# Scan levels further apart in TensorE's order, value weights moved by 192 bytes, one pair of unread products taken out

## The chip, the core and the metric

The kernel runs on one core of a Trainium2 chip. The metric is the device time of one execution in microseconds (us). TensorE (PE) multiplies; VectorE (DVE), ScalarE (ACT) and GpSimd (POOL) do the rest; SyncE (SP) issues most of the DMAs.

## What is computed

One layer of an encoder on a sequence of 512 tokens with 1024 channels, all in float32:

```python
h = rms_norm(x, norm1_g)
u_pool, aq, ak, av, rq, rf, rb, ri, rg, gate_pre = split_cols(h @ w_in)
y_pool = pool_mixer(u_pool)                      # centred means over 2, 4, 8, 16 tokens
y_attn = diff_attention(aq, ak, av, lam)         # 4 heads
y_rec  = hgrn2_mixer(rq, rf, rb, ri, rg)         # two-way gated linear recurrence, 4 heads
x = x + (gates * (y @ w_up), summed over the three) @ w_out
h2 = rms_norm(x, norm2_g)
x = x + (silu(h2 @ w_gate) * (h2 @ w_up)) @ w_ffn_out
out = rms_norm(x, final_norm_g)
```

## The kernel before

**Products.** Every operand of a large product is split into a high and a low part of type float32r (`whi`, `wlo`, `hT_hi`, `hT_lo`), and a product is three terms. Two forms matter here. `cols_mm` holds weights still and streams 512 tokens of hT past them (512 columns in each matmul). `rows_mm` holds hT still and streams 256 columns of weights; it serves the *value* products, `ri` for the recurrence (tile v_rec) and `av` for the attention (va_hi, va_lo). The weights come by DMA into `raw`, are rounded by ACT into `whi` (L180) and subtracted by DVE into `wlo` (L181); both tiles come from the pool `wsp`, three buffers of 4096 bytes each. In the built program's layout the buffers of `wsp` and the tiles of hT begin at the same byte counted modulo 256, namely 32. In the feed-forward layer pads of 192 bytes ahead of the tiles put the streamed operand (the tiles of h2 and of its forms) at 224 and the weights at 32, so the two differ by 64 modulo 256.

**The scan.** `rec_scan(h)` computes one head of the recurrence as a pyramid of levels n = 1, 2, 4, ... 256. At each level PE makes four small float32 products (`rc<-kq,kc`, each two instructions in the trace), then two DVE multiplications (L755) change the queries of `kq` in place, POOL (L758; DVE at the level 128) changes its keys, ACT copies the keys (`kc`, L724), and DVE writes the level's products into the triangle `pt` under a mask (L770). A level's products need the multiplications of the level before.

**What sets the order.** PE's order is fixed when the program is written: `Pipe.run` lets generators yield, counts a nominal PE time for each matmul, and resumes a stream when its nominal time has come. A level of the scan yields ("w", 2.0) or ("w", 1.7): PE is to do that much other work (the projections in `jobs`) before the next level. The heads of the attention wait in the same way for the event AF (their queries and keys are there) and 3.5 more. The other engines' order is made by a scheduler from dependences and its own estimates; they run their queues in order.

**Unread products.** In the feed-forward layer each pair of column blocks j = 1 to 21 is seven products of half size with 256 columns in each matmul. After the first of them the pairs 4 and 12 issue two matmuls of 512 columns into a PSUM bank that nobody reads; the second streams the same weights from 64 bytes further on.

Of the kernel before, what the change touches and what calls it, by code (L numbers as in the profile page):

```python
# [11 lines left out]
F32 = mybir.dt.float32  # L12
# [6 lines left out]
P = 128  # L19
# [57 lines left out]
def encoder_kernel(ctx: ExitStack, tc: tile.TileContext, x, norm1_g, w_in, pool_w, pool_scale,  # L77
# [30 lines left out]
    const = ctx.enter_context(pool("const"))  # L108
    wraw = ctx.enter_context(pool("wraw", 2))
    wsp = ctx.enter_context(pool("wsp", 3))  # L110
    small = ctx.enter_context(pool("small", 6))
    psum = ctx.enter_context(pool("psum", 3, space=PSUM))

    def bank(name, shape=(P, 512)):
# [13 lines left out]
    mhalf = const.tile([P, 8], F32, name="mhalf")  # L128
    nc.vector.memset(mhalf, -0.5)
    masks = const.tile([P, len(LEVELS), P], U8, name="masks")  # L130
    vecs = const.tile([14, P], F32, name="vecs")
    vcol = const.tile([P, 14], F32, name="vcol")
    gain_a = const.tile([P, 1], F32, name="gain_a")
    lb = const.tile([P, 8], F32, name="lb")
# [28 lines left out]
    class Part:  # L163


        def __init__(self, chunk, view, a, b, wpool=None):
            self.chunk, self.view, self.a, self.b, self.wpool = chunk, view, a, b, wpool
            chunk.left += 1

        def ready(self):  # L170
            return True

        def split(self):
            self.hi, self.lo = split_w(self.view(self.chunk.raw), self.a, self.b, self.wpool)
            self.chunk.left -= 1

    def split_w(view, a, b, wpool=None):
        hi = (wpool or wsp).tile([P, a, b], F32R, name="whi")
        lo = (wpool or wsp).tile([P, a, b], F32R, name="wlo")
        nc.scalar.copy(out=hi, in_=view)  # L180
        nc.vector.tensor_tensor(out=lo, in0=view, in1=hi.bitcast(F32), op=ALU.subtract)  # L181
        return hi, lo
# [203 lines left out]
            for j in range(0, n, 2):  # L386
                yield Part(ch, lambda raw, j=j: raw[:, j:j + 2, :], 2, 512, wpool)

    def quarter_parts(w, c0, n, where=None):

        v = w.rearrange("(kt p) c -> p kt c", p=P)
        for c in range(0, n, 256):
            ch = Chunk(v[:, :, c0 + c:c0 + c + 256], KT, 256, where if c == 0 else None)
            yield slice(c, c + 256), [Part(ch, lambda raw, j=j: raw[:, j:j + 4, :], 4, 256) for j in (0, 4)]


    def cols_mm(ps, part, r, nk, sub=0, lo_col=0, n=512, r_lo_last=False):
# [68 lines left out]
    xg = st0.enter_context(pool("xg"))  # L466
    xraw = st0.enter_context(pool("xraw", 3))
    g_b = xg.tile([P, D], F32, name="g1b")
    with tc.issue_after(warmed):
        nc.scalar.dma_start(out=g_b, in_=norm1_g.broadcast_to([P, D]))  # L470
    xt, first_raw = [], []
# [237 lines left out]
    def rec_scan(h):  # L709
# [30 lines left out]
        while n < 256:  # L740
            nb2 = S // (2 * n)
            ps = bank("rc", (P, NB, P))
            for b in range(NB):
                if n <= 64:
                    ks = kc[:, b * P:(b + 1) * P]
                    qs = strided(kq, b * P, [[2 * n, P // (2 * n)], [S + n, 2], [1, n]])
                else:
                    ks = kq[:, 2 + b % 2, b * P:(b + 1) * P]
                    qs = kq[:, 1 - b % 2, (b ^ 1) * P:((b ^ 1) + 1) * P]
                mm(ps[:, b, :], ks, qs, True, True)  # L750

            for off, o in ((0, tstep + 1), (S + n, 0)):
                xv = strided(kq, off, [[2 * n, nb2], [1, n]])
                tv = strided(tot, toff + o, [[2, nb2], [0, n]])
                nc.vector.tensor_tensor(out=xv, in0=xv, in1=tv, op=ALU.mult)  # L755
            xv = strided(kq, 2 * S, [[2 * n, nb2], [S + n, 2], [1, n]])
            tv = strided(tot, toff + 1, [[2, nb2], [tstep - 1, 2], [0, n]])
            (nc.gpsimd if n < 128 else nc.vector).tensor_tensor(out=xv, in0=xv, in1=tv, op=ALU.mult)  # L758
            if n < 64:
                kc = key_copy(2 * n)  # L760
            if n < 128:
                pv = strided(pyr, poff, [[S, 2], [1, nb2]])
                a = strided(tot, toff, [[tstep, 2], [2, nb2]])
                c = strided(tot, toff + 1, [[tstep, 2], [2, nb2]])
                nc.vector.tensor_tensor(out=pv, in0=a, in1=c, op=ALU.mult)
                tot, toff, tstep = pyr, poff, S
                poff += nb2
            if n <= 64:
                m = masks[:, LEVELS.index(n), :].rearrange("p (o t) -> p o t", o=1).to_broadcast([P, NB, P])
                nc.vector.copy_predicated(out=diag, mask=m, data=ps)  # L770
            else:
                nc.scalar.copy(out=strided(pt, P, [[2 * S + 2 * P, 2], [S - P, 2], [1, P]]), in_=ps)
            n *= 2
            yield ("w", 2.0 if n <= 128 else 1.7)
        for d in range(2):
            ps = bank("rc", (P, 2, 256))
            ts = slice(256 * (1 - d), 256 * (1 - d) + 256)
# [17 lines left out]

    cols = {n: col_parts(w_in2, KT, OFF[n] + P, 512 - P, P) for n in ("rq", "rf", "rb")}
    cols["rg"] = col_parts(w_in2, KT, OFF["rg"], 512, P)
    vparts = list(quarter_parts(w_in2, OFF["ri"], 512))

    def add_front(h):  # L800
        for i, n in enumerate(("rq", "rf", "rb")):
# [56 lines left out]
    def att_head(h):  # L858
        if h:
            yield ("e", f"T{h - 1}", 0.0)  # L860
        yield ("e", f"AF{h}", 3.5)
        t = att.pop(h)
        at, (vh, vl), aT, y_attn = ATT["at"], ATT["v"], ATT["aT"], ATT["y"]
        strip = ATT["strip"].tile([P, 896], F32, name="strip")
        nc.sync.dma_start(out=strip, in_=c_dist[h])
        zz = at.tile([P, NB, 2], F32, name="zz")
        rr = at.tile([P, NB, 2], F32, name="rr")
        probs = {}

        def scores(i):  # L870
            bs = slice(i * P, (i + 1) * P)
            mx = small.tile([P, 2], F32, name="mx")
            ex = []
            for c in range(2):
                ps = bank("rc")
                mm(ps, t[f"q{c}"][:, bs], t[f"k{c}"], True, False)
                mm(ps, t[f"q{c}"][:, bs], t[f"l{c}"], False, True)
                s = at.tile([P, S], F32, name=f"s{c}")

                nc.vector.tensor_tensor_reduce(out=s, in0=strip[:, 384 - P * i:896 - P * i], in1=ps, scale=1.0,  # L880
                                               scalar=3.0e38, op0=ALU.add, op1=ALU.min, accum_out=mx[:, c:c + 1])
                nc.scalar.activation(out=s, in_=s, func=AF.Exp, scale=-1.0, bias=mx[:, c:c + 1],  # L882
                                     accum_out=zz[:, i, c:c + 1])
                ex.append(s)

            nc.vector.reciprocal(out=rr[:, i, :], in_=zz[:, i, :])
            co = small.tile([P, 1], F32, name="co")
            nc.vector.scalar_tensor_tensor(out=co, in0=zz[:, i, 0:1], scalar=nlam, in1=rr[:, i, 1:2],
                                           op0=ALU.mult, op1=ALU.mult)
            nc.vector.scalar_tensor_tensor(out=ex[0], in0=ex[1], scalar=co, in1=ex[0], op0=ALU.mult, op1=ALU.add)  # L890
            probs[i] = ex[0]

        def turn(i):
            bs = slice(i * P, (i + 1) * P)
            p = probs.pop(i)
            pt = bank("tp", (P, NB, P))
            for k in range(NB):
                transpose(pt[:, k, :], p[:, k * P:(k + 1) * P], ident)
            nc.scalar.copy(out=aT[0][:, :, bs], in_=pt)
            nc.vector.tensor_tensor(out=aT[1][:, :, bs], in0=pt, in1=aT[0][:, :, bs].bitcast(F32), op=ALU.subtract)  # L900

        scores(0)
        for i in range(NB):
            yield ("w", 2.5)
            if i + 1 < NB:
                scores(i + 1)
            else:
                mark(f"QK{h}")
            yield ("w", 2.1 + (1.0 if i + h == 0 else 0.0))
            if h and i == 0:  # L910
                yield ("e", f"PV{h - 1}", 0.0)
            turn(i)
        mark(f"T{h}")
        yield ("e", "VA", 1.5)
        yield ("w", 1.5)
        ps = bank("rc")
        es = slice(h * P, (h + 1) * P)
        terms = [(vh, aT[0]), (vl, aT[0]), (vh, aT[1])]
        for i, (a, r) in enumerate(terms):
            for k in range(NB):  # L920
                mm(ps, a[:, k, es], r[:, k, :], i == 0 and k == 0, i == 2 and k == NB - 1)
            yield
        mark(f"PV{h}")
        og, rbp = yield from head_norm(ps, at, gain_a, rr[:, :, 0], 1)
        nc.vector.tensor_tensor(out=og, in0=og, in1=rbp, op=ALU.mult)
        nc.scalar.copy(out=y_attn[0][:, h, :], in_=og)
        nc.vector.tensor_tensor(out=y_attn[1][:, h, :], in0=og, in1=y_attn[0][:, h, :].bitcast(F32),
                                op=ALU.subtract)
# [6 lines left out]

    add_att(0)
    add_att(1)
    aparts = list(quarter_parts(w_in2, OFF["av"], 512))
    for i, (cs, parts) in enumerate(aparts):
        jobs.add(parts, values_job(cs, v_att_evac, "VA" if i else None))  # L940
    add_att(2)
# [172 lines left out]
    def ffn_pair_bodies(j):  # L1114
# [3 lines left out]
        def first(part):  # L1118
# [5 lines left out]
            yield from product(c["zy"][:, 0:256], part, 1, f.r21, True)  # L1124


            if j in (4, 12):
                w = part.hi.rearrange("p n k c -> p (n k c)")
                for skip in (0, 16):
                    mm(bank("tp"), w[:, 0:P], w[:, skip:skip + 512], True, True)  # L1130
# [241 lines left out]
```

## Time and profile before

| | us |
|---|---|
| median of 3 runs | 913.66 (913.07 to 913.75) |
| the profiled execution | 913.64 |
| its span, first to last instruction | 911.9 |

| part of the span (us) | what PE does |
|---|---|
| 38 to 215 | scans of the recurrence among projections; value products `ri` at 92 to 128 |
| 230 to 380 | attention among projections; value products `av` at 241 to 269 |
| 380 to 568 | pooling branch, up projections, output projection |
| 568 to 783 | feed-forward, first part (256 columns) |
| 783 to 904 | feed-forward, second part (512 columns) |

PE is busy for 889.2 us of the span, and its granted clock is 1.00 in all stretches but the last. A busy PE is read further by how often a matmul starts, since matmuls overlap: in a row of the timeline the second number is the time to the end of the group, and the pace is the distance from the start of one group to the start of the next, divided by the count.

### The profile page before, as it was taken

To read this page: it belongs to the slowest core of one execution; us is meant where nothing else is said; L and a number is where in the kernel's file an instruction comes from. 1 tells how busy PE (TensorE), PEld (TensorE's weight loads), DVE (VectorE), ACT (ScalarE), POOL (GpSimd) and SP (SyncE) were. 2 spreads that over 40 slices of the span, in tenths; PEclk is the share of its full clock that TensorE was granted. 3 is DMA by queue.
4 is the path that set the end of the run, shared out by engine and by line. 5 is a ranking of instruction groups with operands and counts; after the bars stand their busy time and mean duration, and the time that the engine had idled before them with its cause. 6 is when DMAs were issued, how large, how long until landed. Compare 5 with 4: busy or idle time off the path is not lost. (4 is left out here: it accounts for less than half of the span.)

```text
span 911.9 us, 13179 instructions
## 1 busy us (share of the span) xinstructions
PE 889.2 (98%) x5357; PEld 783.6 (86%) x5357; DVE 582.0 (64%) x876; ACT 420.7 (46%) x652; POOL 62.0 (7%) x62
## 2 busy tenths in 40 slices
PE   6999999999999999999999999999999999999996
PEld 5977987887898888778888898999999999888885
DVE  5696553663867765654325554998887888644544
ACT  5544423433655674332233424755655556533433
POOL 2233311210000000000000000000000000000000
PEclk9999999999999999999999999999999999999999
DMA  8322030314033213523334350153433434323312
GB/s 244 106 69 70 3 91 25 114 47 154 26 112 91 89 52 117 185 79 96 97 122 147 102 153 0 48 139 94 137 95 104 128 94 133 122 70 105 111 39 93
DMA packets 106313, 89.01 MB, mean 98 GB/s; under 512 B 2686, under 2 KB 93324, under 8 KB 106124
## 3 DMA queue, kind: packets, MB, share of 16 engines
q1 hardware_dynamic: 105532, 86.59, 31.0%
q10 hardware_dynamic: 720, 1.57, 0.5%
q8 instruction: 42, 0.69, 0.3%
q14 instruction: 19, 0.16, 0.1%
HBM read 86.06 MB, written 2.10 MB: 97 GB/s over the span
## 5 line engine op out<-in xcount | busy, mean ns | idle before, releaser
L181 DVE TENSOR_TENSOR wlo<-raw,whi 128x1024 fp32r<-128x1024 f32 (+1 forms) x146 | 170.2, 1169 | 165.5 <-PE mm L90 85.0
L180 ACT CAST whi<-raw 128x1024 fp32r<-128x1024 f32 (+1 forms) x146 | 143.7, 990 | 207.5 <-PE mm L90 122.1
L90 PE MATMUL mm<-hT_hi,whi 128*128 128x512 f32 (+1 forms) x440 | 110.7, 389 | 0.0
L90 PE MATMUL mm<-hT_hi,wlo 128*128 128x512 f32 (+1 forms) x440 | 108.3, 383 | 0.0
L90 PE MATMUL mm<-hT_lo,whi 128*128 128x512 f32 (+1 forms) x440 | 107.9, 382 | 0.0
L90 PEld LDWEIGHTS mm<-hT_hi,whi 128*128 128x128 f32 x440 | 79.2, 191 | 16.0 <-issue 1.9
L90 PEld LDWEIGHTS mm<-hT_lo,whi 128*128 128x128 f32 x440 | 79.2, 188 | 15.0
L90 PEld LDWEIGHTS mm<-hT_hi,wlo 128*128 128x128 f32 x440 | 78.9, 188 | 15.4 <-issue 1.0
L299 DVE TENSOR_TENSOR slo<-sums,shi 128x1024 fp32r<-128x1024 f32 x42 | 51.1, 1217 | 0.2 <-ACT shi L297 0.2
L297 ACT CAST shi<-sums 128x1024 fp32r<-128x1024 f32 x42 | 44.2, 1052 | 2.0 <-DVE sums L261 1.5
L758 POOL TENSOR_TENSOR kq<-kq,pyr 128x512 f32<-128x512 f32 x24 | 33.4, 1392 | 46.4 <-ACT kc L724 29.9
L90 PEld LDWEIGHTS rc<-kq,kc 128*128 128x128 f32 x224 | 29.7, 191 | 6.7 <-issue 2.4
L90 PE MATMUL rc<-kq,kc 128*128 128x128 f32 x224 | 32.1, 287 | 2.9 <-DVE kq L755 2.9
L755 DVE TENSOR_TENSOR kq<-kq,pyr 128x256 f32<-128x256 f32 x56 | 26.1, 507 | 13.1 <-PE rc L90 13.0
L724 ACT COPY kc<-kq 128x512 f32<-128x512 f32 x28 | 18.7, 667 | 30.1 <-POOL kq L758 19.0
L882 ACT ACTIVATE s<-s,mx 128x512 f32<-128x512 f32 x32 | 23.0, 720 | 16.2 <-DVE mx L880 16.0
L90 PE MATMUL mm<-fhi,slo 128*128 128x256 f32 x168 | 26.2, 278 | 0.5 <-DVE slo L299 0.5
L90 PE MATMUL mm<-y_hi,whi 128*128 128x512 f32 x96 | 26.4, 393 | 0.0
L90 PE MATMUL mm<-y_lo,whi 128*128 128x512 f32 x96 | 26.2, 392 | 0.0
L90 PE MATMUL mm<-fhi,shi 128*128 128x256 f32 x168 | 26.1, 277 | 0.1
L90 PE MATMUL mm<-flo,shi 128*128 128x256 f32 x168 | 25.9, 276 | 0.0
L90 PE MATMUL mm<-y_hi,wlo 128*128 128x512 f32 x96 | 25.9, 390 | 0.0
(255 smaller groups left out, 1812.0 us busy)
## 6 DMA issues: line engine op xcount, KB each, us to landing
raw<-in_w_ffn_in_dram SPq DMA_DIRECT2D x44, 512.0 KB, 5.2
raw<-in_w_in_dram SPq DMA_DIRECT2D x18, 1024.0 KB, 5.1
raw<-in_w_in_dram SPq DMA_DIRECT2D x24, 512.0 KB, 4.1
raw<-in_w_ffn_out_dram SPq DMA_DIRECT2D x10, 1024.0 KB, 5.1
raw<-in_w_out_dram SPq DMA_DIRECT2D x4, 1024.0 KB, 5.4
xin<-in_x_dram SPq DMA_DIRECT2D x4, 512.0 KB, 9.4
raw<-in_w_up_rec_dram SPq DMA_DIRECT2D x2, 1024.0 KB, 7.9
x<-in_x_dram SPq DMA_DIRECT2D x1, 2048.0 KB
```

The costliest lines, as they stand in the source:

```text
L90: i = nc.tensor.matmul(out_, lhsT=lhsT, rhs=rhs, start=start, stop=stop, skip_group_check=chain)
L180: nc.scalar.copy(out=hi, in_=view)
L181: nc.vector.tensor_tensor(out=lo, in0=view, in1=hi.bitcast(F32), op=ALU.subtract)
L297: nc.scalar.copy(out=hi, in_=view)
L299: on_dve = nc.vector.tensor_tensor(out=lo, in0=view, in1=hi.bitcast(F32), op=ALU.subtract).ins
L724: nc.scalar.copy(out=strided(kc, 0, [[2 * n, S // (2 * n)], [n, 2], [1, n]]), in_=strided(kq, 2 * S, [[2 * n, S // (2 * n)], [S + n, 2], [ ...
L755: nc.vector.tensor_tensor(out=xv, in0=xv, in1=tv, op=ALU.mult)
L758: (nc.gpsimd if n < 128 else nc.vector).tensor_tensor(out=xv, in0=xv, in1=tv, op=ALU.mult)
L882: nc.scalar.activation(out=s, in_=s, func=AF.Exp, scale=-1.0, bias=mx[:, c:c + 1], accum_out=zz[:, i, c:c + 1])
```

## The change

The levels of the scan yield 2.7 and 2.4 in the place of 2.0 and 1.7, and the heads of the attention 4.4 behind AF in the place of 3.5. The tiles of `wsp` get 1088 elements (4352 bytes, 17 times 256), and the value weights are written 192 bytes into them, so that they begin at 224 modulo 256; all others stay at 32. To make room, `vecs` moves from the constants to a pool of the first stage and the pool `small` keeps five buffers. All tiles behind move by 768 bytes, three times 256, so no other distance modulo 256 changes. The unread pair at j = 12 goes; the one at j = 4 stays.

```diff
-    small = ctx.enter_context(pool("small", 6))
+    small = ctx.enter_context(pool("small", 5))
...
-    vecs = const.tile([14, P], F32, name="vecs")
...
-    def split_w(view, a, b, wpool=None):
-        hi = (wpool or wsp).tile([P, a, b], F32R, name="whi")
-        lo = (wpool or wsp).tile([P, a, b], F32R, name="wlo")
+    def split_w(view, a, b, wpool=None, skip=0):
+
+        n, k = a * b, skip // 4
+        hi, lo = ((wpool or wsp).tile([P, n if wpool else 1088], F32R, name=name)[:, k:k + n]
+                  .rearrange("p (a b) -> p a b", a=a) for name in ("whi", "wlo"))
...
+    vecs = xg.tile([14, P], F32, name="vecs")
...
-            yield ("w", 2.0 if n <= 128 else 1.7)
+            yield ("w", 2.7 if n <= 128 else 2.4)
...
-    vparts = list(quarter_parts(w_in2, OFF["ri"], 512))
+    vparts = list(quarter_parts(w_in2, OFF["ri"], 512, None, 192))
...
-        yield ("e", f"AF{h}", 3.5)
+        yield ("e", f"AF{h}", 4.4)
...
-    aparts = list(quarter_parts(w_in2, OFF["av"], 512))
+    aparts = list(quarter_parts(w_in2, OFF["av"], 512, None, 192))
...
-            if j in (4, 12):
+            if j == 4:
```

In PE's order of the first head, from the products of level 2 to those of level 8, it was:

```order
L90 MATMUL rc<-kq,kc 128x128 x4
L90 MATMUL mm<-hT_lo,whi 128x512 x2
L90 MATMUL mm<-hT_hi,wlo 128x512 x8
L90 MATMUL rc<-kq,kc 128x128 x4
L90 MATMUL mm<-hT_hi,whi 128x512 x8
L90 MATMUL mm<-hT_lo,whi 128x512 x2
L90 MATMUL rc<-kq,kc 128x128 x4
```

and is now:

```order
L90 MATMUL rc<-kq,kc 128x128 x4
L90 MATMUL mm<-hT_hi,wlo 128x512 x6
L90 MATMUL mm<-hT_hi,whi 128x512 x8
L90 MATMUL rc<-kq,kc 128x128 x4
L90 MATMUL mm<-hT_lo,whi 128x512 x8
L90 MATMUL mm<-hT_hi,wlo 128x512 x6
L90 MATMUL rc<-kq,kc 128x128 x4
```

Between two levels there stood ten matmuls of 512 columns, and now there are fourteen. On DVE the same place, from the multiplications behind level 2 to those behind level 4 (`f`, `kq` by `om` and `kq` from `q` belong to the next head), was:

```order
L755 TENSOR_TENSOR kq<-kq,pyr 128x128x2 x2
L770 COPY_PREDICATED pt<-masks,rc 128x4x128
L765 TENSOR_TENSOR pyr<-pyr 128x2x32
L181 TENSOR_TENSOR wlo<-raw,whi 128x1024
L661 TENSOR_SCALAR f<-f,om,lb 128x512
L755 TENSOR_TENSOR kq<-kq,pyr 128x64x4 x2
```

and is now:

```order
L758 TENSOR_TENSOR kq<-kq,pyr 128x128x2 x2
L773 COPY_PREDICATED pt<-masks,rc 128x4x128
L182 TENSOR_TENSOR wlo<-raw,whi 128x1024
L768 TENSOR_TENSOR pyr<-pyr 128x2x32
L664 TENSOR_SCALAR f<-f,om,lb 128x512
L666 TENSOR_SCALAR kq<-kq,om 128x512
L723 TENSOR_TENSOR kq<-q,f 128x512
L758 TENSOR_TENSOR kq<-kq,pyr 128x64x4 x2
```

Two instructions more stand ahead of the level's multiplications. The first scores of the attention (`rc<-k,q` and `rc<-l,q`) stood in PE's order so, each name with its number:

```order
L90 MATMUL mm<-hT_lo,whi 128x512 x8
L90 MATMUL mm<-hT_hi,wlo 128x512 x2
L90 MATMUL rc<-k_1865,q_1863 128x512
L90 MATMUL rc<-l_1867,q_1863 128x512
L90 MATMUL rc<-k_1866,q_1864 128x512
L90 MATMUL rc<-l_1868,q_1864 128x512
```

and now stand so:

```order
L90 MATMUL mm<-hT_lo,whi 128x512 x8
L90 MATMUL mm<-hT_hi,wlo 128x512 x6
L90 MATMUL rc<-k_1865,q_1863 128x512
L90 MATMUL rc<-l_1867,q_1863 128x512
L90 MATMUL rc<-k_1866,q_1864 128x512
L90 MATMUL rc<-l_1868,q_1864 128x512
```

They come four matmuls of 512 columns later. Behind the attention's value products all orders are as before, but for the unread pair and a place or two on DVE and ACT.

## Rows read from the trace of the kernel before

**Rows 1.** The page, busy us (share of the span) and instructions of PE.

```profile
PE 889.2 (98%) x5357; PEld 783.6 (86%) x5357; DVE 582.0 (64%) x876; ACT 420.7 (46%) x652; POOL 62.0 (7%) x62
```

**Rows 2.** Waits of PE, whole span: us in total, times, longest.

```profile
PE rc L90 <- DVE kq L755: 3.5, 5, 1.0
...
PE rc L90 <- DVE kq L758: 1.4, 1, 1.4
```

**Rows 3.** Timeline, 49 to 180 us, PE: start, us to the group's end, instruction.

```profile
49.97 0.61 PE L90 MATMUL mm<-hT_lo,whi 128*128 128x512 f32 x2
...
51.06 1.13 PE L90 MATMUL rc<-kq,kc 128*128 128x128 f32 x8 [0.47 <-DVE kq L755]
...
64.76 1.13 PE L90 MATMUL rc<-kq 128*128 128x128 f32 x8 [0.52 <-DVE kq L755]
...
69.14 1.97 PE L90 MATMUL rc<-kq 128*128 128x256 f32 x8 [1.41 <-DVE kq L758]
...
89.71 1.13 PE L90 MATMUL rc<-kq,kc 128*128 128x128 f32 x8 [0.87 <-DVE kq L755]
...
116.34 1.13 PE L90 MATMUL rc<-kq,kc 128*128 128x128 f32 x8 [1.00 <-DVE kq L755]
...
179.18 1.20 PE L90 MATMUL rc<-kq,kc 128*128 128x128 f32 x8 [0.59 <-DVE kq L755]
```

**Rows 4.** Timeline, 47 to 68 us, DVE and POOL.

```profile
47.63 0.23 DVE L765 TENSOR_TENSOR pyr<-pyr 128x64 f32<-128x64 f32 x1 [0.40 <-POOL kq L758]
...
47.77 1.22 DVE L181 TENSOR_TENSOR wlo<-raw,whi 128x1024 fp32r<-128x1024 f32 x1
...
48.91 1.33 DVE L661 TENSOR_SCALAR f<-f,om,lb 128x512 f32<-128x512 f32 x1
...
50.16 0.75 DVE L755 TENSOR_TENSOR kq<-kq,pyr 128x256 f32<-128x256 f32 x2
...
65.11 1.52 POOL L758 TENSOR_TENSOR kq<-kq,pyr 128x512 f32<-128x512 f32 x1 [0.79 <-ACT kc L724]
...
65.15 2.57 DVE L181 TENSOR_TENSOR wlo<-raw,whi 128x1024 fp32r<-128x1024 f32 x1
```

**Rows 5.** Groups of DVE by form, 38 to 128 us: count; busy us, mean ns; idle.

```profile
L770 DVE COPY_PREDICATED pt<-masks,rc 128x512 f32<-128x512 uint8 x19 | 13.9, 730 | 0.0
...
L663 DVE TENSOR_SCALAR kq<-kq,om 128x512 f32<-128x512 f32 x4 | 1.9, 473 | 0.0
...
L720 DVE TENSOR_TENSOR kq<-q,f 128x512 f32<-128x512 f32 x2 | 1.4, 678 | 0.0
```

**Rows 6.** Timeline, 231 to 233 us, PE.

```profile
231.88 0.39 PE L90 MATMUL rc<-k,q 128*128 128x512 f32 x1
232.92 0.50 PE L90 MATMUL rc<-l,q 128*128 128x512 f32 x1 [0.66 <-DVE l L848]
```

**Rows 7.** Groups of PE by form (count; busy us, mean ns), then timeline, 254 to 260 us.

```profile
L90 PE MATMUL mm<-whi,hT_hi 128*128 128x256 f32 x128 | 19.0, 286 | 0.0
...
254.68 1.12 PE L90 MATMUL mm<-wlo,hT_hi 128*128 128x256 f32 x8
...
259.48 0.60 PE L98 MATMUL tp<-ident,s 128*128 128x128 f32 x4
```

**Rows 8.** The chain that ended last: start, us, matmuls (256 columns; 512 in the last row).

```profile
599.30 1.41 PE rc L90 x12
...
613.44 1.41 PE rc L90 x12
...
616.69 1.36 PE rc L90 x12
...
690.13 1.36 PE rc L90 x12
691.96 1.37 PE mm L90 x12
...
844.30 4.08 PE mm L90 x18
```

More of the change, by code (lines that the diff above doesn't have):

```diff
@@ L163, in encoder_kernel, with __init__ @@
     class Part:
-        def __init__(self, chunk, view, a, b, wpool=None):
-            self.chunk, self.view, self.a, self.b, self.wpool = chunk, view, a, b, wpool
+        def __init__(self, chunk, view, a, b, wpool=None, skip=0):
+            self.chunk, self.view, self.a, self.b, self.wpool, self.skip = chunk, view, a, b, wpool, skip
             chunk.left += 1
@@ L173, in split @@
         def split(self):
-            self.hi, self.lo = split_w(self.view(self.chunk.raw), self.a, self.b, self.wpool)
+            self.hi, self.lo = split_w(self.view(self.chunk.raw), self.a, self.b, self.wpool, self.skip)
             self.chunk.left -= 1
-    def split_w(view, a, b, wpool=None):
-        hi = (wpool or wsp).tile([P, a, b], F32R, name="whi")
-        lo = (wpool or wsp).tile([P, a, b], F32R, name="wlo")
+    def split_w(view, a, b, wpool=None, skip=0):
+        n, k = a * b, skip // 4
+        hi, lo = ((wpool or wsp).tile([P, n if wpool else 1088], F32R, name=name)[:, k:k + n]
+                  .rearrange("p (a b) -> p a b", a=a) for name in ("whi", "wlo"))
         nc.scalar.copy(out=hi, in_=view)
@@ L387, in row_parts, with quarter_parts @@
                 yield Part(ch, lambda raw, j=j: raw[:, j:j + 2, :], 2, 512, wpool)
-    def quarter_parts(w, c0, n, where=None):
+    def quarter_parts(w, c0, n, where=None, skip=0):
         v = w.rearrange("(kt p) c -> p kt c", p=P)
@@ L393, in quarter_parts @@
             ch = Chunk(v[:, :, c0 + c:c0 + c + 256], KT, 256, where if c == 0 else None)
-            yield slice(c, c + 256), [Part(ch, lambda raw, j=j: raw[:, j:j + 4, :], 4, 256) for j in (0, 4)]
+            yield slice(c, c + 256), [Part(ch, lambda raw, j=j: raw[:, j:j + 4, :], 4, 256, None, skip)
+                                       for j in (0, 4)]
     def cols_mm(ps, part, r, nk, sub=0, lo_col=0, n=512, r_lo_last=False):
```

## The prediction

> **What bounds the kernel now.** I read the busy line first: PE is busy for 889.2 of 911.9 us [rows 1], so a change pays only where PE stands still or where its matmuls follow each other more slowly than they could. The waits come next. Leaving aside the start of the program, two lines of them stand out, 3.5 and 1.4 us [rows 2]: six places in the scan where PE is ready for a level's products and DVE has not yet multiplied kq. The timeline shows them one by one, 0.47, 0.52, 1.41, 0.87, 1.00 and 0.59 us, 4.86 together [rows 3]. One more stands at the first scores of the attention [rows 6]. Then the pace. Matmuls of 512 columns start every 0.227 us (4.08 by 18) [rows 8]. Those of 256 columns have three paces: the value products 120.0 ns (4.80 us for 40 matmuls, five groups of eight, of which the first and the end stand in the rows) [rows 7], and the feed-forward either 117.6 (1.41 us for 12) or 113.4 (1.36 for 12) [rows 8]. The granted clock stands at full speed in all of them, so the paces aren't the clock.
>
> **Part 1, levels further apart.** What a wait costs is more than its idle time, since the matmul before drains alone. At 49.97 us two matmuls of 0.227 us should let the next group start at 50.42; it starts at 51.06, so 0.64 us are lost where 0.47 are shown [rows 3]. With 0.165 more at each of six places the scan loses 4.86 + 0.99 = 5.85 us.
>
> The new order puts four more matmuls of 512 columns between two levels, 4 x 0.227 = 0.91 us, in most gaps (two more in some, and as much nominal time among the value products). A wait shorter than that goes: five of six, all but 1.41 us, of which 0.50 stays. What fills the gap is work that PE has to do anyway, so the longer gap costs nothing as long as projections are left; the last head's scan ends, in the new order, with its transposes, and 70 matmuls of 512 columns (16 us) still follow before the attention's first scores, so the cover lasts.
>
> The new place of each instruction counts too. DVE's queue now has two more instructions ahead of the multiplications behind level 4. I follow that place from the start of level 2's products. Their eight instructions take 0.9 us, the multiplications start 0.2 later and take 0.75 [rows 4], the masked copy 0.73, wlo 1.22, pyr 0.23, f 1.33 (as long as in the row, where POOL ran beside it), the key 0.47, the query 0.68, the multiplications 0.75, and 0.2 to reach PE: 7.5 us [rows 4, 5]. Level 8 stands two gaps later in PE's order, 2 x (0.9 + 14 x 0.227) = 8.2 us. In the old order two gaps were 2 x (0.9 + 10 x 0.227) = 6.3. So this place, which waited for 0.47 us, gets 0.7 us to spare, even with the two instructions. Nine stretches between levels now hold 2.4 to 3.2 us of such foreign work (by the same durations), against six before; they fit by the same sum, unless POOL's work stretches them further: a wlo of 1.22 us took 2.57 where POOL ran L758 beside it [rows 4]. For that I keep 0.2 us. The levels pass POOL's queue too: three reciprocal roots of head_norm now stand behind a key update of 1.52 us [rows 4]; their transposes come 3.55 nominal us after the sums on PE, which holds one update and the root, and would show as a wait on rso if not. So from 5.85 us, 0.66 stay (0.50 with its drain) and 0.2 are new: **5.0 us** come back, with bounds of 0 and 5.85.
>
> **Part 2, the attention's first scores.** At 231.88 us one matmul should take 0.227 us; the next starts at 232.92, so 0.81 us are lost [rows 6]. The scores now come four matmuls, 0.91 us, later. **0.8 us** come back (0 to 0.81). What is late next is the softmax of the first block, which PE's transposes follow at the same distance as before.
>
> **Part 3, value weights 192 bytes further.** Three forms like the row, with 128 matmuls each, are 384 [rows 7]. At 120.0 ns they stand at equal bytes modulo 256. The feed-forward matmuls have the distance of 64 that the value products get, and run at 113.4 or 117.6 ns [rows 8]. So the bounds are 384 x 2.4 ns = 0.9 us and 384 x 6.6 ns = 2.5 us. The feed-forward keeps either pace until something interrupts it, and the value products are interrupted at every level and every block of scores, so that they should get some of both; I take the middle, **1.7 us**. The writes of ACT and DVE into the moved tiles keep their shapes, so I cost them at nothing; they lie beside PE in any case. The Trainium skill speaks against this part: SBUF — State Buffer, "SBUF: two separate sides", says that PE has its own ports and that its accesses never wait on anyone. By that rule the three paces cannot come from where an operand lies. The trace agrees that something other than the clock sets them, and shows no single run in which only an address changes; the first rival takes this up.
>
> **Part 4, one unread pair less.** It stands between the end of one twelve at 691.49 us (690.13 + 1.36) and the next at 691.96: **0.47 us** [rows 8]. The pace is the fast one on both sides (1.36 and 1.37 us per 12), so the pair at j = 12 finds it and changes nothing. At j = 4, at 615 us, it goes from 1.41 to 1.36 us per 12 [rows 8]; that pair stays. The move of vecs and the fifth buffer of small are off PE's path: vecs is read once, in the first stage, and five buffers are still more than the two blocks in flight. All cost nothing, or show up as a wait on ms, mx or co.
>
> **The sum.** The profiled execution took 913.64 us, within 0.02 of the median of the runs (913.66), so I use its own time: 913.64 - 5.0 - 0.8 - 1.7 - 0.47 = **905.7 us**.
>
> **The rivals.**
> *A: the shift does nothing.* The value products stay at 120 ns, as they would where the pace came from the shape or the neighbours of a matmul. For it: no row changes the address alone. Against it: the value products, at distance 0, run at 120, and the feed-forward with the same shape and distance 64 doesn't. The time is 905.7 + 1.7 = 907.4 us. This is where the skill's rule on ports would lead.
> *B: new waits take the place of the old ones.* DVE's queue has more foreign work ahead of the multiplications, and the scheduler that puts it there goes by estimates that don't know POOL's stretching of wlo. If the scan goes on losing its 5.85 us, the time is 913.64 - 0.8 - 1.7 - 0.47 = 910.7 us. Against it is the 0.7 us to spare worked out above.
> *C: the feed-forward loses its fast pace.* If the pair at j = 4 leaves PE at the slow pace, nothing sets it right at j = 12 any more. From 615 to 783 us at 1.41 instead of 1.36 us per 12, that is 168 x 3.7% = 6.2 us, and the time is 911.9 us. For it: the slow pace did last, from 599 to 615 us, until the pair came [rows 8]. Against it: both pairs of this trace are followed by the fast pace.
> *D, slower: DVE as the scan's bound.* In each of the nine filled stretches POOL may stretch wlo by 1.35 us (2.57 for 1.22 [rows 4]) and a second instruction by about as much; less the 0.7 us to spare that is up to 2.0 us each. The other parts give 3.0 us, so it makes the kernel slower from 5.85 + 3.0 = 8.85 us lost in the scan, 1.0 at each of the nine; at 1.25 each it loses 11.2 and the time is 913.64 + 11.2 - 5.85 - 3.0 = 916.0 us. Against it: of six stretches as full in the old order, not all waited, and with less room.
>
> **How the numbers follow.** My forecast, with 0.70 for it, has its own range from 903.0 (all of 5.85 and 0.81, 2.5, 0.47, and 0.6 more where the slow stretch of 17 us at 598 to 615 turns fast: 10.2 us, with 0.4 for smaller drains that show no idle time) to 909.4 (half of part 1, half of part 2, 0.9, 0.47). A has 0.08, B 0.12, C 0.06, D 0.04. The range from 903.0 to 910.8 takes in A and B and leaves out C, D and a little of the forecast's edge. A measurement of this kernel can tell about 0.2%, 1.8 us, from no change: below 911.8 is faster, which holds the forecast, A, B and a little of C, 0.91; the rest of C is the same, 0.05; D is slower, 0.04.
>
> **What would show it.** Part 1: PE's waits for kq fall from 4.9 us to below 1.2, and PE's starts around the levels show no gap. Part 2: no wait for l at the first scores. Part 3: value products start every 113 to 118 ns, never steadily every 120. Part 4: the stretch from 616 to 783 us is shorter by 0.47 us at an unchanged 113 to 114 ns. The prediction is wrong if waits for kq stay above 3 us (B), if twelve feed-forward matmuls take 1.41 us behind j = 4 (C), or if the value products keep 120 ns (A).

## The result, and the profile after

The changed kernel takes 904.84 us (median of 5 runs: 904.26, 904.65, 904.84, 905.19 and 911.67) against 913.66 us; the ratio on record is 0.988 with an interval from 0.984 to 0.993 (that of the two medians is 0.990). A second series gave 904.92 us (median of 12) and 0.9905, from 0.987 to 0.994. The forecast was 905.7 us, so the usual run is 0.9 us better than said. But the profiled execution took 911.67 us, outside the range, and it isn't an accident of that one run: the times of both kernels stand in two groups with nothing between.

| kernel | lower group | upper group |
|---|---|---|
| before, 89 runs | 66 runs, 912.7 to 915.7, mean 913.9 | 23 runs, 920.4 to 921.9, mean 921.0 |
| changed, 17 runs | 12 runs, 904.3 to 905.2, mean 904.7 | 5 runs, 911.7 to 912.0, mean 911.8 |

In either group the change is worth 9.1 to 9.2 us (by medians and by means), and the groups lie 7.1 us apart in both kernels. Each median above is that of a lower run; below, kernels are compared group with group.

PE's waits in the whole span, after the change (engine, tile and line, what was waited for: us in total, times, longest), are these, and the page's busy line stands under them:

```profile
PE tp L98 <- DVE hrow L432: 7.3, 1, 7.3
PE rc L98 <- DVE hrow L432: 1.4, 1, 1.4
PE mm L90 <- DVE slo L300: 0.4, 1, 0.4
```

```profile
PE 893.1 (98%) x5355; PEld 790.3 (87%) x5355; DVE 576.9 (63%) x876; ACT 420.8 (46%) x652; POOL 57.4 (6%) x62
```

The first two belong to the start of the program. The kq lines of [rows 2] are gone altogether. PE is busy for 3.9 us longer than in [rows 1], though the span is 2 us shorter: it works at a slower pace somewhere. Two places in the timeline (start, us to the group's end, instruction) tell how much had been gained by then: the first scores, which answer [rows 6], and, from the profile before and then after, the attention's first products with the values.

```profile
225.45 0.39 PE L90 MATMUL rc<-k,q 128*128 128x512 f32 x1
225.68 0.41 PE L90 MATMUL rc<-l,q 128*128 128x512 f32 x1
```

```profile
273.08 1.07 PE L90 MATMUL rc<-aT_hi,va_hi 128*128 128x512 f32 x4
```

```profile
264.43 0.84 PE L90 MATMUL rc<-aT_hi,va_hi 128*128 128x512 f32 x3
```

The third score comes 231.88 - 225.45 = 6.4 us sooner, the fourth 7.2 us, without a wait, and the values' products 8.65 us. By 265 us nearly everything has been gained. The value products, which answer [rows 7], show two paces in turn:

```profile
85.11 1.08 PE L90 MATMUL mm<-whi,hT_hi 128*128 128x256 f32 x8
86.02 1.07 PE L90 MATMUL mm<-whi,hT_lo 128*128 128x256 f32 x8
...
88.74 1.11 PE L90 MATMUL mm<-whi,hT_hi 128*128 128x256 f32 x8
89.68 1.11 PE L90 MATMUL mm<-whi,hT_lo 128*128 128x256 f32 x8
```

Eight take 0.91 us (114 ns each) in the first stretch between two levels and 0.94 us (118 ns) in the next. The loss is further on, in the feed-forward. Around its last wait, and then in the chain that ended last (start, us, matmuls; it answers [rows 8]):

```profile
590.49 0.74 PE L90 MATMUL mm<-fhi,slo 128*128 128x256 f32 x4 [0.38 <-DVE slo L300]
```

```profile
591.23 1.41 PE rc L90 x12
...
605.36 1.41 PE rc L90 x12
607.24 1.41 PE mm L90 x12
...
690.62 1.41 PE rc L90 x12
...
781.07 1.41 PE mm L90 x12
782.49 4.08 PE rc L90 x18
```

Twelve take 1.41 us ahead of the unread pair (606.6 us), behind it, and to the end at 782 us, where before they went to 1.36 at the pair. This is the stretch that rival C described. Over 191 us the slow pace costs 191 x 0.05 / 1.41 = 6.8 us, the distance between the groups within the rounding of the rows.

### The profile page after: what moved, and what is told of

It is laid out like the page before. It is cut to its first block, busy times and chain, and to the rows that moved or that the text cites. A ratio compares the mean times of both kernels' runs of the same rounds, so it can differ in the third digit from the quotient of the medians.

```text
span 909.9 us, 13175 instructions
## 1 busy us (share of the span) xinstructions
PE 893.1 (98%) x5355; PEld 790.3 (87%) x5355; DVE 576.9 (63%) x876; ACT 420.8 (46%) x652; POOL 57.4 (6%) x62
## 5 line engine op out<-in xcount | busy, mean ns | idle before, releaser
L758 DVE TENSOR_TENSOR kq<-kq,pyr 128x256 f32<-128x256 f32 x56 | 23.7, 463 | 24.3 <-PE rc L90 24.2
L761 POOL TENSOR_TENSOR kq<-kq,pyr 128x512 f32<-128x512 f32 x24 | 29.7, 1236 | 59.6 <-ACT kc L727 44.3
L1154 DVE TENSOR_TENSOR g<-mm,g 128x256 f32<-128x256 f32 x21 | 8.9, 423 | 28.5 <-PE mm L90 28.5
```

Of the source, the lines that this page charges most:

```text
L1154: on_dve = nc.vector.tensor_tensor(out=c["g"], in0=c["x"], in1=c["g"], op=ALU.add).ins
```

## The experiments

What was open: which edit gave how much, why the waits went further than the arithmetic said, whether the address sets the pace, and what makes the feed-forward slow in some runs and not in others.

**1. The shift undone.**

```diff
-    vparts = list(quarter_parts(w_in2, OFF["ri"], 512, None, 192))
+    vparts = list(quarter_parts(w_in2, OFF["ri"], 512, None, 0))
...
-    aparts = list(quarter_parts(w_in2, OFF["av"], 512, None, 192))
+    aparts = list(quarter_parts(w_in2, OFF["av"], 512, None, 0))
```

> The changed kernel with the value weights back at the start of their buffers (the third part of the change undone, nothing else). If the distance between the start bytes of the two operands sets the pace, the value products run at 120 ns again in the steady stretches, where the changed kernel has 113 and 118; by the mean of its trace (116.2 ns against 119.5 before) that costs 384 x 3.3 ns = 1.3 us, so about 906.1 us, and the scan stays free of waits for kq. If the neighbours or the new order set the pace (rival A), the products keep 113 to 118 ns and the time stays at 904.8 us.

Measured: a lower group of five runs, mean 905.6 us, 0.9 us above the changed kernel's 904.7, and one run at 912.7. Its timeline, at the place of the rows above:

```profile
89.29 1.12 PE L90 MATMUL mm<-whi,hT_hi 128*128 128x256 f32 x8
90.25 1.12 PE L90 MATMUL mm<-whi,hT_lo 128*128 128x256 f32 x8
```

Eight take 0.96 us, 120 ns each. Nothing but the start byte differs (every engine runs the same instructions in the same order in both traces), so the address sets the pace and rival A falls. The Trainium skill (SBUF — State Buffer, "SBUF: two separate sides") says that PE doesn't wait on other users of this memory; what the prediction drew from it, that the paces can't come from where an operand lies, goes beyond that rule and doesn't hold here: the measurement decides. The gain is 0.9 us by the times and 1.6 by the traces (the values' products start at 266.01 instead of 264.43 us; in three more traces with the shift they start at 264.17 to 264.24). The times are the weaker of the two, since the changed kernel ran on other chips than this one. On this chip stand experiments 4 and 5, the changed kernel with one unread pair more and one less, at 904.7 and 903.7; halfway between them, at 904.2, the gain by the times is an estimated 1.4 us.

**2. The levels alone.**

```diff
-            yield ("w", 2.0 if n <= 128 else 1.7)
+            yield ("w", 2.7 if n <= 128 else 2.4)
```

> The kernel before with the levels of the scan further apart (2.7 and 2.4 in place of 2.0 and 1.7) and no other edit. If spacing alone returns the waits, PE's six waits for kq (4.9 us of idle time) fall below 0.5 us and the first scores of the attention come 5.0 to 5.9 us sooner than at 231.4 us; the time is then 913.7 - 5.0 to 5.9 = 907.8 to 908.7 us, and the wait for l at the first scores (0.66 us) stays, since nothing here moves them. If the waits went for another reason (the shift, fewer buffers, the moved vector), this kernel stays at 913.7 us with its waits. If the feed-forward's pace after the unread pair at j = 4 is a matter of chance, this kernel has a second pair at j = 12 to come back by.

Measured, as an edit of the kernel before: seven runs with a mean of 907.2 us, 6.6 us below the 913.8 of the kernel before beside them, and five runs near 914.0. Its waits of PE past the start, and the scores of [rows 6]:

```profile
PE rc L90 <- DVE l L848: 0.7, 1, 0.7
PE mm L90 <- DVE slo L299: 0.5, 1, 0.5
```

```profile
225.72 0.39 PE L90 MATMUL rc<-k,q 128*128 128x512 f32 x1
226.76 0.50 PE L90 MATMUL rc<-l,q 128*128 128x512 f32 x1 [0.66 <-DVE l L848]
```

No wait for kq is left; the third score comes 231.88 - 225.72 = 6.16 us sooner. The wait for l stands as in [rows 6], so that the second part is what takes it away: 0.8 us. In this profiled execution (914.1 us) the feed-forward was slow from 593 us to its end, although both pairs, at j = 4 and j = 12, stand in this kernel: the twelve behind the first of them, at 609.22 us, and the twelve behind the second, at 688.82, take 1.41 us.

**3. Half the step.**

```diff
-            yield ("w", 2.0 if n <= 128 else 1.7)
+            yield ("w", 2.35 if n <= 128 else 2.05)
```

> The kernel before with the levels half as much further apart (2.35 and 2.05 in place of 2.0 and 1.7) and no other edit. By the working of the prediction each added matmul takes 0.227 us from every wait: with two more per gap the waits of 0.47, 0.52, 1.41, 0.87, 1.00 and 0.59 us become 0.02, 0.07, 0.96, 0.42, 0.55 and 0.14, so 2.1 us of idle time stay and 2.7 us (2.7 of the idle time and next to none of the drains) come back: 911.0 us against the 907.3 us of the usual runs with the full step. If the waits go because other work changes place on DVE and PE, and not matmul by matmul, they vanish at the half step too and the time is near 907.5 us; if the half step falls short of the whole way from level to level, hardly anything comes back and it stands at 913 us.

Measured: nine runs with a mean of 908.2 us (5.5 us gained, where the working gives 2.7) and three near 915.4. One line of waits for kq is left, three places of 0.16, 0.33 and 0.17 us:

```profile
PE rc L90 <- DVE kq L755: 0.7, 3, 0.3
```

Two matmuls more took away even the wait of 1.41 us. DVE's timeline of this kernel ahead of that level says how, and PE's row for the level stands at its end:

```profile
67.50 0.76 DVE L755 TENSOR_TENSOR kq<-kq,pyr 128x256 f32<-128x256 f32 x2
68.18 0.68 DVE L758 TENSOR_TENSOR kq<-kq,pyr 128x512 f32<-128x512 f32 x1
69.63 1.23 DVE L181 TENSOR_TENSOR wlo<-raw,whi 128x1024 fp32r<-128x1024 f32 x1 [0.77 <-issue]
```

```profile
69.84 1.89 PE L90 MATMUL rc<-kq 128*128 128x256 f32 x8
```

In the kernel before, the wlo of 2.57 us [rows 4] stood ahead of these multiplications; here one stands behind them, and they end a microsecond before PE needs them. (Another, of 2.43 us, now stands one level earlier, at 61.96 us, and leaves a wait of 0.16 there.) So the wait went because a foreign instruction changed its place in DVE's queue, and the arithmetic of one matmul after the other falls. In the changed kernel a wlo stands ahead of the last level again (POOL, DVE and PE, by start):

```profile
67.38 1.55 POOL L761 TENSOR_TENSOR kq<-kq,pyr 128x512 f32<-128x512 f32 x1 [1.89 <-ACT kc L727]
68.45 1.56 DVE L182 TENSOR_TENSOR wlo<-raw,whi 128x1024 fp32r<-128x1024 f32 x1 [0.47 <-issue]
...
72.39 0.68 DVE L761 TENSOR_TENSOR kq<-kq,pyr 128x512 f32<-128x512 f32 x1
...
73.22 1.97 PE L90 MATMUL rc<-kq 128*128 128x256 f32 x8
```

The multiplications end at 73.07 us and PE takes them at 73.22 without a wait: here the full step is just long enough. The wlo takes 1.56 us, not the 2.57 of [rows 4], where POOL's update of kq began within 0.04 us of it; here that one is 1.07 us ahead. In both places wlo is longer than its usual 1.22 us by about as much as POOL's update still had to run: 1.35 us longer with 1.48 to run, 0.34 longer with 0.48. Rival D's price shrinks with that.

**4. The pair at j = 12 put back.**

```diff
-            if j == 4:
+            if j in (4, 12):
```

> The changed kernel with the unread pair at j = 12 put back (the fourth part of the change undone, nothing else). If the pair only costs its own time, every run is 0.47 us longer than the usual 904.7 us of the changed kernel: 905.2 us. If it gives the feed-forward a second chance to take the fast pace, a run that goes slow behind j = 4 (1.41 us for 12 matmuls, as in the profiled run of the changed kernel, 911.7 us) comes back at about 692 us and ends near 908.5 us, so that no run stands at 911 us or above. If the pair has nothing to do with the pace, runs near 911.5 to 912 us are as frequent as before, about one in five.

Measured: five runs with a mean of 904.7 us and one at 912.4. A run at 1.41 us per 12 that came back to 1.36 at j = 12 would stand near 908.5; there is none, neither here nor among the 89 runs of the kernel before, which has this pair too. In no run on record does the pair at j = 12 rescue the quick pace.

**5. No pair at all.**

```diff
-            if j == 4:
+            if j < 0:
```

> The changed kernel without any unread pair in the feed-forward (the one at j = 4 left out too, which changes no result). If the pair at j = 4 is what brings the fast pace, all runs keep the slow pace from about 590 to 783 us, 1.41 instead of 1.36 us for 12 matmuls, which is 168 us x 3.7% = 6.2 us on top of 904.7 - 0.5 us: 910.4 us in every run. If the pace is taken by chance at the start of the feed-forward and the pair changes nothing, most runs stand at 904.2 us and some at 910 to 911 us.

Measured: five runs with a mean of 903.7 us and one at 911.3. The pair at j = 4 isn't what brings the quick pace at this distance; most runs have it without any pair. Against experiment 4, on the same chip, two pairs cost 904.7 - 903.7 = 1.0 us, 0.5 each: the fourth part's price.

**6. The changed kernel again.**

> The changed kernel as it is, beside the other runs. If the feed-forward takes one of two paces by chance at its start, near 590 us, and keeps it (1.36 or 1.41 us for 12 matmuls over some 190 us), its runs stand in two groups 6 to 7.5 us apart, near 904.7 and 911.7 us, and nothing between, and the profiled run tells which group it belongs to. If the slow profiled run was an accident of that one, all six stand within 1 us of 904.7.

Measured: eight runs from 904.3 to 905.1, four from 911.7 to 912.0. This time the profiled run was a lower one (904.4 us). The same wait at 590 us, and what follows it in the chain:

```profile
590.34 0.74 PE L90 MATMUL mm<-fhi,slo 128*128 128x256 f32 x4 [0.46 <-DVE slo L300]
```

```profile
591.08 1.36 PE rc L90 x12
...
604.68 1.36 PE rc L90 x12
606.50 1.37 PE mm L90 x12
```

Same program, same order, same addresses: 1.41 us behind a wait that ended at 590.49, and 1.36 behind one that ended at 590.34. Already ahead of this wait the two traces differ (the changed kernel's first profile, then this one):

```profile
588.54 0.64 PE L90 MATMUL rc<-fhi,slo 128*128 128x256 f32 x4
589.01 0.63 PE L90 MATMUL mm<-fhi,shi 128*128 128x256 f32 x4
```

```profile
588.36 0.62 PE L90 MATMUL rc<-fhi,slo 128*128 128x256 f32 x4
588.81 0.62 PE L90 MATMUL mm<-fhi,shi 128*128 128x256 f32 x4
```

Four take 0.47 us (118 ns each) in the first and 0.45 (113) in the second. But the wait doesn't simply hand the pace on: in experiment 1 the same matmuls go at 118 ns ahead of it and at 113 behind it, in the kernel before and in experiment 2 at 113 ahead and 118 behind. After this wait PE waits for no other engine until the feed-forward ends, and in these two traces the pace doesn't change any more.

**7. Other distances, on the value products.** One shift for each half of either product, in two runs; the first is shown.

```diff
-            yield slice(c, c + 256), [Part(ch, lambda raw, j=j: raw[:, j:j + 4, :], 4, 256, None, skip)
+            yield slice(c, c + 256), [Part(ch, lambda raw, j=j: raw[:, j:j + 4, :], 4, 256, None, skip[c // 256])
...
-    vparts = list(quarter_parts(w_in2, OFF["ri"], 512, None, 192))
+    vparts = list(quarter_parts(w_in2, OFF["ri"], 512, None, (128, 64)))
...
-    aparts = list(quarter_parts(w_in2, OFF["av"], 512, None, 192))
+    aparts = list(quarter_parts(w_in2, OFF["av"], 512, None, (224, 160)))
```

> The changed kernel with four shifts of the value weights in place of one: 128 and 64 bytes for the two halves of the recurrence's values, 224 and 160 for those of the attention, so that the moving operand starts 128, 192, 32 and 96 bytes (modulo 256) before the stationary one instead of 64. If any distance but 0 gives the two paces of 113 and 118 ns, all four halves show both, as at 64, and the time is that of the changed kernel. If the pace goes by the distance itself, the halves differ: one may hold 113 ns without ever taking 118 (it is then a place to put the feed-forward's operands), another may stand at 120 like distance 0.

> As the run with four shifts (32, 96, 128 and 192 bytes of distance, of which none held 113 ns), with 240 and 208 bytes for the halves of the recurrence's values and 176 and 144 for those of the attention: distances of 16, 48, 80 and 112. If 64 is the one distance with the pace of 113 ns, these four stand between 115 and 120 ns and none shows a steady 113. If a neighbour of 64 (48 or 80) holds 113 ns and never takes 118, it is the better place for every product of 256 columns.

Measured, as the mean from start to start over 87 to 93 products for each distance (bytes modulo 256; distance 0 from experiment 1, 357 products), pairs that start 130 ns or more apart left out as interruptions:

| distance | 0 | 16 | 32 | 48 | 80 | 96 | 112 | 128 | 192 |
|---|---|---|---|---|---|---|---|---|---|
| ns | 119.5 | 117.2 | 118.2 | 119.2 | 119.0 | 118.3 | 117.5 | 118.7 | 117.8 |

None of them holds 113; on the value products 64 alone shows it (the changed kernel's mean, of both paces, is 116.2). In all kernels here the stationary operand begins at 32 modulo 256, so these runs can't tell the distance from the start byte of the streamed operand itself. The whole kernels took 905.07 and 905.28 us in their single runs. At 192 the pace is one, 117.8 ns, behind every level, as in the first of the two runs:

```profile
100.88 1.10 PE L90 MATMUL mm<-whi,hT_lo 128*128 128x256 f32 x8
101.82 1.10 PE L90 MATMUL mm<-wlo,hT_hi 128*128 128x256 f32 x8
...
104.60 1.10 PE L90 MATMUL mm<-whi,hT_lo 128*128 128x256 f32 x8
105.54 1.10 PE L90 MATMUL mm<-wlo,hT_hi 128*128 128x256 f32 x8
```

**8. The feed-forward at 192 bytes.** A distance that seemed to have one pace alone should leave one group of times.

```diff
-    pad(h2p, 192, "h2_a")
+    pad(h2p, 64, "h2_a")
...
-    pad(h2p, 64, "h2_b")
+    pad(h2p, 192, "h2_b")
...
-            pad(pool_, 192, "forms_a")
+            pad(pool_, 64, "forms_a")
```

> The changed kernel with the feed-forward's moving operands 128 bytes earlier in memory, so that they stand 192 bytes before the stationary ones instead of 64; the value products keep their 64. At 192 the values held one pace only, 118 ns. If the two groups of times (904.3 to 905.1 and 911.7 to 912.0) are the two paces that 64 bytes of distance allow in the feed-forward, this kernel has 117.7 ns throughout from 590 to 783 us and one group of times, near 911.8 us, with nothing near 904.7. If the groups come from something else, both are still there, 7 us apart.

Measured: six runs from 905.3 to 906.1 and six from 911.1 to 911.9. The expectation of one group fell. The chain of the profiled run (905.3 us) shows where the quick pace comes from here:

```profile
602.75 2.83 PE mm L90 x24
605.58 1.41 PE rc L90 x12
607.45 1.36 PE mm L90 x12
608.81 1.36 PE rc L90 x12
```

All of the stretch from 576 us on is slow, and between 605.58 + 1.41 and 607.45 stands the unread pair.

**9. The same without the pair.**

```diff
-            if j == 4:
+            if j < 0:
```

> The kernel with the feed-forward at 192 bytes of distance and without the unread pair at j = 4 (which changes no result). In the run with the pair the matmuls went at 117.7 ns from 576 to 607 us, every draw of them, and at 113.3 ns behind the pair; its times were two groups of six, near 905.6 and 911.5 us. If it is the pair that turns the slow pace into the fast one there, in about half of the runs, this kernel has 117.7 ns up to 783 us and one group, 911.5 - 0.5 = 911.0 us in every run. If the two groups are drawn elsewhere and the pair only happened to stand there, there are still runs near 905.2 us.

Measured: six runs of six from 911.0 to 912.1. There is one group, and it is the upper one. If half of this kernel's runs were quick without the pair, six in a row in the upper group would come once in 64 times; and beside it, on the same chip, the next experiment's kernel, which has pairs, is quick in six runs of ten. So the two groups are the two paces of the feed-forward, shown by taking one of them away. At this distance the pair makes the quick pace, in about half of the runs.

**10. The same with four pairs.**

```diff
-            if j == 4:
+            if j in (4, 5, 6, 7):
```

> The kernel with the feed-forward at 192 bytes of distance and the unread pair at j = 4, 5, 6 and 7 in place of j = 4 alone. If each pair turns the slow pace fast with about even chance and leaves the fast pace alone (as every pair that met it so far), 15 runs in 16 end fast: three more pairs cost 3 x 0.47 us, a run that turns at the second pair loses 0.5 us more, so most stand at 907.0 to 908.0 us and at most one run near 913 us. If what the first pair finds decides for all that follow (the slow pace stands in the same relation to the next pair), half of the runs are still slow, at 911.5 + 1.4 = 912.9 us.

Measured: six runs from 906.9 to 907.6 and four from 911.7 to 912.9. The first expectation, at most one run in the upper group, falls. The share of that group is near the second's half, but its reason, that the first pair decides for those that follow, falls with the trace. The chain on either side of the four pairs, in a run of 906.9 us:

```profile
605.04 1.41 PE rc L90 x12
606.91 1.36 PE mm L90 x12
...
615.07 1.36 PE rc L90 x12
616.90 1.42 PE mm L90 x12
...
625.38 1.41 PE rc L90 x12
627.25 1.41 PE mm L90 x12
...
635.73 1.41 PE rc L90 x12
637.61 1.36 PE mm L90 x12
```

Slow to quick, quick to slow, slow to slow, slow to quick: in these four meetings and the one of experiment 8, a pair at 192 bytes draws the pace anew, and may lose it as well as find it. At 64 bytes, in the traces of all kernels here, a pair that met the quick pace left it so nine times of nine, and one that met the slow pace turned it once in four times (the kernel before, [rows 8]; not the changed kernel, nor the kernel of experiment 2 at j = 4 and at j = 12).

**11. The version to keep.** Experiment 5's kernel once more.

> The changed kernel without the unread pair at j = 4, once more and with more runs, as the version to keep. If the pair only draws the pace once more at a distance of 64 bytes, this kernel is 0.5 us faster than the changed one in each group (near 904.1 and 911.3 us), and the share of slow runs stays near that of the changed kernel (5 of 17) or of the kernel before (about 3 in 10). If the pair rescues many runs that were drawn slow near 590 us, the share of slow runs rises clearly above that, to half or more.

Measured: five runs with a mean of 903.8 us and one at 911.1. With experiment 5 that is 10 lower runs of 903.3 to 904.2 us and 2 upper ones, 0.9 us below the changed kernel's group. Of this, 0.46 us is the pair that can be seen (606.61 to 607.07 us in the changed kernel); the rest isn't placed, and the two kernels ran on different chips. Beside the kernel before the ratio is 0.9906, from 0.988 to 0.993. It beats both kernels, by little over the changed one.

## Why the prediction was right, and where it was wrong

**Part 1 was right in kind and too small.** 5.0 us were forecast; alone it gives 6.2 by its trace and 6.6 by its times. Two terms failed. The words "all but 1.41 us, of which 0.50 stays" took a wait to be worth the matmuls put in front of it. The half step shows that the order of DVE's queue counts for more: 0.45 us per gap removed 1.41 at one place. And the 0.2 us for new waits behind a stretched wlo did not come. The ceiling of 5.85 was too low by 0.3 to 0.7 us as well; the 0.4 us for drains without idle time, which the prediction kept in its range and left out of the term, would make up for it, but no run shows that they did. Rivals B and D fall with the empty line of waits for kq.

**Part 2 was right:** 0.8 us, seen in the fourth score, which waits in experiment 2 and in none of the kernels with AF at 4.4.

**Part 3 was right in kind;** its size, 1.7 us, agrees with the traces (1.6 to 1.8), while the times leave it between 0.9 and 1.4. The products take both paces, as said, and more of the slow than of the quick one in the attention. Rival A's 120 ns stand only where the shift is undone.

**Part 4 was right in its price,** 0.47 us, and wrong in its reason. "At j = 4, at 615 us, it goes from 1.41 to 1.36 us per 12 [rows 8]; that pair stays" reads one trace in which a draw at j = 4 happened to go well. Experiment 5 has the quick pace with no pair.

**The sum** of the measured parts, 6.2 to 6.6, 0.8, 0.9 to 1.8 and 0.5, is 8.4 to 9.7 us, and 9.1 to 9.2 were gained in either group, where 8.0 were forecast. The usual run came out 0.9 us lower than said, inside the forecast's own range.

**The step that failed is the feed-forward's pace, which the sum carried over from one trace at no price, and rival C with its 0.06.** The sum took the quick pace behind j = 4 as settled by the pair; measured, 1.41 us per 12 lasts from 591 to 782 us in the profiled run, and the 5 runs of 17 in its group take 7.1 us more than the others. Rival C's time was right, 911.9 us worked out and 911.7 to 912.0 measured, but partly by luck: it put 6.2 us on a base of 905.7, and 7.1 on 904.7 were measured. Its mechanism was half right: the slow pace does pass the pair at j = 4. But it was made to hang on the missing pair at j = 12, and the kernel before, which has that pair, is slow in 23 runs of 89, 7.1 us above its others, with no run halfway. The pace is drawn anew in every run of both kernels, and the shares, 5 of 17 and 23 of 89, don't show that the change touches that. A range for one execution had to reach 912 us; and a row of one trace ("both pairs of this trace are followed by the fast pace") could not bear the weight it was given. The one row that spoke for chance, 1.41 us per 12 from 599 to 615 us at unchanged addresses [rows 8], was priced as an edge of the forecast.

**What stays open:** what it is at the end of the wait at 590 us that decides the pace (the two traces differ in when DVE's slo ends, by 0.15 us, and in the pace ahead of the wait, but experiment 1 and the kernel before change their pace there); and why the share of upper runs differs between series (7 of 17, 8 of 23, 6 of 17, then 1 of 16 and 0 of 11 for the kernel before). Each of these series ran on another chip, so the share may go by the chip; no run here separates the two.

## What to carry to other kernels

When an engine waits for another now and then, look at what stands ahead of the awaited instruction in that engine's queue: a foreign 2.6 us there is worth more than the matmuls that one can put in front of the wait. Where the same instruction shows two paces in one trace, suspect that it is drawn, and run the kernel a dozen times before pricing an edit by one profile; compare group with group. And an instruction kept because it "resets" something should be tried with the good state in front of it, with the bad one, and left out altogether.

## What the hardware showed that was not expected

- The start byte of the streamed operand, modulo 256 and with the stationary one at 32, sets the pace of 256-column matmuls at an unchanged granted clock (1.00): 120 ns at distance 0, 117 to 119 as the mean at eight others on the value products, and at 64 either 113.3 or 117.7.
- At 64 the pace lasts as long as nothing interrupts: 191 us of 1.41 us per 12 in one run and of 1.36 in the next, from the same program.
- At 192 the restarts behind waits gave 117.7 ns each time (so in the trace of experiment 9, whose six runs without a pair took 911.0 to 912.1 us), and yet two matmuls of 512 columns can bring 113.3 ns there, and the next two can lose it.
